# Softmax statistics of two heads side by side in one two-column tile

## The chip, the core and the metric

The kernel runs on one core of a Trainium2 chip. The metric is the device time of one execution in microseconds. TensorE does the matrix products and transposes, VectorE and ScalarE the elementwise work, GpSimd a part of the splits explained below, and SyncE issues the transfers.

## The reference

Two layers work on 256 latent and 256 context tokens of width 1024. Each layer normalises its input, projects it, runs a pooling mixer, a window attention and a global attention, gates and merges the three branches, and ends with a gated MLP. Both attentions have 8 query heads of 64 on 2 key heads. What matters here is the softmax. The window attention has one more logit per head, the sink, which takes part in the maximum and in the sum and has no value:

```python
s_snk = jnp.broadcast_to(sink_l, s_lat.shape[:-1] + (1,))
p = jax.nn.softmax(jnp.concatenate([s_lat, s_ctx, s_snk], axis=-1), axis=-1).astype(v.dtype)
```

The global attention has a plain softmax. Latent queries read latent and context keys, context queries only context keys; the context has no attention of its own in the second layer.

## The kernel before

Matrix products are done in three passes over numbers split into a high and a low part (`mm3`, lines 204 to 207); weights arrive by DMA, ScalarE makes the high part (line 188), GpSimd or VectorE the low part (line 190).

Attention works in units. A unit is one head of one block of 128 queries, and units stand in the order block, key head, `par`, `j`, so that two neighbours (`j` = 0 and 1) are two heads of the same key head and half. They share one tile of split probabilities, and the values are multiplied for both at once. A latent unit has 512 keys, a context unit 256. Layer 0 has 32 units per attention (16 latent, 16 context), layer 1 has 16.

For each unit, `scores` (line 859) makes the scores in a PSUM bank `S` with two products (and a mask product of `triB` for latent window units), takes the negated maximum `nm` on VectorE (line 873), in window attention scales it and takes the smaller of it and the negated sink (line 875), and makes the exponentials `pr` with their row sum `ls` on ScalarE (line 878), in window attention also the sink's exponential `es` (line 883). `finish` (line 886) adds the sink's exponential (line 891), takes the reciprocal `rl` (line 893) and normalises `pr`, on ScalarE for each fourth unit (line 895), otherwise on VectorE (line 897). `turn` (line 899) transposes `pr` on TensorE into `ptp` (line 908) and splits it into `pH` and `pL`; `values` (line 911) multiplies the values of a pair into `O` (line 922).

`S` has two banks, the pool of transposes two, `pr` shares a pool of six tiles, and the small tiles `nm`, `ls`, `es`, `rl` have three buffers each.

`slots` (line 938) lays the steps out in time: slot i holds the scores of unit i and the finish of unit i - 1, then the transposes of unit i - 2 and, each second slot, the values of an earlier pair. `attention` (line 1089) puts other products (the pooling projection, gates, branch projections) between the halves of the slots. From this written order a list scheduler with estimated durations makes the final order of each engine, which is fixed when the program is built. Each engine then works through its own list in order and waits at an instruction whose inputs are not there.

## Time and profile before

| | |
|---|---|
| runs | 1361.81, 1359.25, 1361.93 us, median 1361.81 |
| profiled execution | 1359.41 us, of it the span from first to last instruction 1357.6 us |
| TensorE busy | 1286.9 us, 95% |
| VectorE busy | 900.2 us, 66% |
| ScalarE busy | 661.9 us, 49% |
| GpSimd busy | 568.3 us, 42% |

Shares of the whole span are means over stages that differ; the attention stages take some 280 of the 1357.6 us. Matmuls are pipelined, so that two that follow each other overlap in the busy time. A wait is time in which an engine stood at its next instruction.

### The profile page before, as it was taken

What the parts mean: (1) busy time and instruction counts of PE and PEld (TensorE: products, weight loads), DVE (VectorE), ACT (ScalarE), POOL (GpSimd) and SP (SyncE); (2) the same over time, 40 slices, a digit from 0 to 9 for tenths busy, and PEclk for the clock granted to TensorE, in tenths of its full rate; (3) what the DMA queues carried; (4) which work ended last, traced back from release to release, by engine and by line L of the source; (5) the groups of instructions that cost most, each with busy time, mean ns of one, the idle gap of its engine ahead of it and who ended that gap; (6) DMA issues with size and microseconds to landing.
All of it is one profiled execution on the core that took longest, in us unless ns stands there. A gap on an engine that the chain in (4) does not pass through costs nothing. (4 is left out here: it accounts for less than half of the span.)

```text
span 1357.6 us, 20919 instructions
## 1 busy us (share of the span) xinstructions
PE 1286.9 (95%) x7845; PEld 1125.6 (83%) x7845; DVE 900.2 (66%) x1822; ACT 661.9 (49%) x1216; POOL 568.3 (42%) x317
## 2 busy tenths in 40 slices
PE   4999999999999999999999999998999998999997
PEld 3877778878788888888788788988888888999997
DVE  6879975878767786777755344477847775656522
ACT  5557762557633344333433223456745764555542
POOL 4322223642244425433343443454235325566663
PEclk8999999999999999999999999999999999999999
DMA  9711215432246525644555455544234326577653
GB/s 283 245 40 63 74 51 157 124 94 94 78 153 188 152 82 168 189 141 154 172 171 169 163 163 167 156 140 159 71 107 149 111 78 186 162 212 217 209 173 100
DMA packets 174087, 195.72 MB, mean 144 GB/s; under 512 B 6879, under 2 KB 147831, under 8 KB 173729
## 3 DMA queue, kind: packets, MB, share of 16 engines
q1 hardware_dynamic: 173088, 193.23, 46.0%
q0 software_dynamic: 896, 1.14, 0.4%
q8 instruction: 62, 1.02, 0.3%
q14 instruction: 41, 0.33, 0.1%
HBM read 191.21 MB, written 3.15 MB: 143 GB/s over the span
## 5 line engine op out<-in xcount | busy, mean ns | idle before, releaser
L190 POOL TENSOR_TENSOR wL<-raw,wH 128x1024 fp32r<-128x1024 f32 (+2 forms) x233 | 539.9, 2322 | 741.5 <-ACT wH L188 672.2
L188 ACT ACTIVATE wH<-raw 128x1024 fp32r<-128x1024 f32 (+2 forms) x294 | 293.2, 1001 | 291.2 <-PE gp L206 163.2
L205 PE MATMUL gp<-hH,wH 128*128 128x512 f32 (+1 forms) x1168 | 396.1, 342 | 6.8 <-DVE fa L1257 3.4
L207 PE MATMUL gp<-hH,wL 128*128 128x256 f32 (+1 forms) x1168 | 392.1, 337 | 1.9 <-POOL wL L190 1.4
L206 PE MATMUL gp<-hL,wH 128*128 128x512 f32 (+1 forms) x1168 | 392.2, 337 | 1.8 <-DVE hL L472 1.8
L205 PEld LDWEIGHTS gp<-hH,wH 128*128 128x128 f32 x1168 | 222.3, 191 | 29.6 <-issue 3.4
L207 PEld LDWEIGHTS gp<-hH,wL 128*128 128x128 f32 x1168 | 222.6, 191 | 25.7 <-POOL wL L190 2.5
L206 PEld LDWEIGHTS gp<-hL,wH 128*128 128x128 f32 x1168 | 223.1, 191 | 23.5 <-DVE hL L472 3.3
L433 DVE SCALAR_TENSOR_TENSOR mb<-raw,cs,mb 128x512 f32<-128x512 f32 x196 | 140.7, 751 | 108.5 <-DMA raw<-in_w_mod_dram 107.5
L205 PE MATMUL gp<-g,wH 128*128 128x256 f32 (+1 forms) x396 | 127.3, 322 | 2.4 <-DVE fa L1257 2.4
L206 PE MATMUL gp<-g,wH 128*128 128x256 f32 (+1 forms) x396 | 126.3, 319 | 0.0
L207 PE MATMUL gp<-g,wL 128*128 128x256 f32 (+1 forms) x396 | 126.3, 319 | 0.0
L190 DVE TENSOR_TENSOR wL<-raw,wH 128x1024 fp32r<-128x1024 f32 (+2 forms) x61 | 71.1, 1169 | 74.6 <-ACT wH L188 74.5
L205 PEld LDWEIGHTS gp<-g,wH 128*128 128x128 f32 x396 | 74.5, 188 | 8.9 <-issue 1.6
L207 PEld LDWEIGHTS gp<-g,wL 128*128 128x128 f32 x396 | 74.6, 188 | 6.0
L206 PEld LDWEIGHTS gp<-g,wH 128*128 128x128 f32 x396 | 74.6, 188 | 5.8
L878 ACT ACTIVATE pr<-S,nm 128x512 f32<-128x512 f32 (+1 forms) x96 | 59.4, 619 | 37.0 <-DVE nm L873 15.5
L873 DVE TENSOR_REDUCE nm<-S 128x1 f32<-128x512 f32 (+1 forms) x96 | 56.9, 593 | 21.5 <-PE S L867 12.7
L205 PE MATMUL gp<-y,wH 128*128 128x512 f32 (+1 forms) x192 | 66.7, 349 | 3.5 <-ACT gt L1023 1.5
L206 PE MATMUL gp<-y,wH 128*128 128x512 f32 (+1 forms) x192 | 65.3, 341 | 0.0
L207 PE MATMUL gp<-y,wL 128*128 128x512 f32 (+1 forms) x192 | 65.1, 339 | 0.0
L202 DVE TENSOR_TENSOR pL<-ptp,pH 128x512 fp32r<-128x512 f32 (+1 forms) x96 | 57.0, 596 | 11.1 <-ACT pH L201 10.3
(214 smaller groups left out, 2208.7 us busy)
## 6 DMA issues: line engine op xcount, KB each, us to landing
raw<-in_w_mod_dram SPq DMA_DIRECT2D x80, 512.0 KB, 3.7
raw<-in_w_gate_dram SPq DMA_DIRECT2D x48, 512.0 KB, 3.5
raw<-in_w_ff_gate_dram SPq DMA_DIRECT2D x44, 512.0 KB, 4.2
raw<-in_w_ff_val_dram SPq DMA_DIRECT2D x44, 512.0 KB, 4.4
raw<-in_w_ff_down_dram SPq DMA_DIRECT2D x44, 512.0 KB, 3.6
raw<-in_w_in_dram SPq DMA_DIRECT2D x32, 384.0 KB, 3.2
raw<-in_w_branch_dram SPq DMA_DIRECT2D x24, 512.0 KB, 3.5
raw<-in_w_mod_dram SPq DMA_DIRECT2D x32, 256.0 KB, 5.9
```

What stands on the lines that cost most here:

```text
L188: h = act.activation(out=self.H, in_=self.raw, func=AF.Copy)
L190: lo = eng.tensor_tensor(out=self.L, in0=self.raw, in1=self.H.bitcast(F32), op=ALU.subtract)
L202: dve.tensor_tensor(out=Lo, in0=src, in1=H.bitcast(F32), op=ALU.subtract)
L205: recent.append(pe.matmul(o, lhsT=aH, rhs=bH, start=first, stop=False))
L206: pe.matmul(o, lhsT=aH, rhs=bL, start=False, stop=False)
L207: pe.matmul(o, lhsT=aL, rhs=bH, start=False, stop=last)
L433: dve.scalar_tensor_tensor(out=S["a"][s], in0=raw, scalar=cs[:, s, k:k + 1], in1=S["a"][s], op0=ALU.mult, op1=ALU.add)
L873: dve.tensor_reduce(out=nm, in_=S, axis=AX.X, op=ALU.max, negate=True)
L878: act.activation(out=pr[:, :nkey], in_=S, func=AF.Exp, scale=0.125 if self.window else 1.0, bias=nm, accum_out=ls)
```

## The change

Statistics are kept for two neighbouring units at a time: `nm`, `ls` and `es` are tiles of two columns, one column per unit.

In window attention the first unit of a pair stops after its maximum. After the second unit's maximum, one SCALAR_TENSOR_TENSOR scales both columns and takes the smaller of them and the two negated sinks; then both exponentials are issued, and the sink exponentials of both are made as one VectorE addition and one exponential. Before, the sink was the bias of the exponential. In global attention each unit's exponential is issued at its own maximum as before.

The finish of a pair is issued once, in the slot after the second unit's scores: one addition (window only), one reciprocal of two columns, in place, and the two normalisations. Transposes and values stay in their slots.

```diff
@@ -869,28 +869,38 @@
                 if msk:
                     ob = (1 - t) * P
                     pe.matmul(S[:, ob:ob + P], lhsT=identb, rhs=triB[:, t], start=False, stop=True)
-                nm = small(1, "nm", 3)
-                dve.tensor_reduce(out=nm, in_=S, axis=AX.X, op=ALU.max, negate=True)
+                if j == 0:
+                    self.two = small(2, "nm", 3), small(2, "ls", 3), [], []
+                nm, ls, prs, Ss = self.two
+                dve.tensor_reduce(out=nm[:, j:j + 1], in_=S, axis=AX.X, op=ALU.max, negate=True)
+                prs.append(tmp(name="pr"))
+                Ss.append(S)
                 if self.window:
-                    dve.tensor_scalar(nm, nm, 0.125, nsink[:, l, h:h + 1], op0=ALU.mult, op1=ALU.min)
-                pr = tmp(name="pr")
-                ls = small(1, "ls", 3)
-                act.activation(out=pr[:, :nkey], in_=S, func=AF.Exp, scale=0.125 if self.window else 1.0, bias=nm,
-                               accum_out=ls)
-                es = None
+                    if j == 0:
+                        return
+
+                    dve.scalar_tensor_tensor(out=nm, in0=nm, scalar=0.125, in1=nsink[:, l, h - 2:h + 1:2],
+                                             op0=ALU.mult, op1=ALU.min)
+                for q in range(2) if self.window else (j,):
+                    act.activation(out=prs[q][:, :nkey], in_=Ss[q], func=AF.Exp, scale=0.125 if self.window else 1.0,
+                                   bias=nm[:, q:q + 1], accum_out=ls[:, q:q + 1])
                 if self.window:
-                    es = small(1, "es", 3)
-                    act.activation(out=es, in_=nm, func=AF.Exp, bias=sinkP[:, l, h:h + 1])
-                self.st[i] = (pr, ls, es)
+                    es = small(2, "es", 3)
+                    dve.tensor_tensor(out=es, in0=nm, in1=sinkP[:, l, h - 2:h + 1:2], op=ALU.add)
+                    act.activation(out=es, in_=es, func=AF.Exp)
+                    self.two += (es,)
+                if j == 1:
+                    self.st[i - 1], self.st[i] = self.two, self.two
 
             def finish(self, i):
                 t, kv, par, j = self.units[i]
                 nkey = self.dims(t)[1] * P
-                pr, ls, es = self.st[i]
-                if self.window:
-                    dve.tensor_tensor(out=ls, in0=ls, in1=es, op=ALU.add)
-                rl = small(1, "rl", 3)
-                dve.reciprocal(rl, ls)
+                ls, prs = self.st[i][1:3]
+                if j == 0:
+                    if self.window:
+                        dve.tensor_tensor(out=ls, in0=ls, in1=self.st[i][4], op=ALU.add)
+                    dve.reciprocal(ls, ls)
+                pr, rl = prs[j], ls[:, j:j + 1]
                 if i % 4 in ANORMS:
                     act.activation(out=pr[:, :nkey], in_=pr[:, :nkey], func=AF.Copy, scale=rl)
                 else:
@@ -899,7 +909,7 @@
             def turn(self, i):
                 t, kv, par, j = self.units[i]
                 lat, nkt, koff = self.dims(t)
-                pr = self.st.pop(i)[0]
+                pr = self.st.pop(i)[2][j]
                 if j == 0:
                     self.st["p", i // 2] = [atile([P, 4, 2, P], F32R, f"p{x}", 2) for x in "HL"]
                 pH, pL = self.st["p", i // 2]
@@ -942,8 +952,8 @@
                     a, b = [], []
                     if i < n:
                         a.append(lambda i=i: self.scores(i))
-                    if 1 <= i <= n:
-                        a.append(lambda i=i: self.finish(i - 1))
+                    if i >= 2 and i % 2 == 0 and i <= n:
+                        a.append(lambda i=i: (self.finish(i - 2), self.finish(i - 1)))
                     if 2 <= i <= n + 1:
                         b.append(lambda i=i: self.turn(i - 2))
                     if i >= 4 and i % 2 == 0:
```

The number of TensorE, GpSimd and SyncE instructions is unchanged. VectorE has 72 instructions fewer and ScalarE 24. The final order differs only in the attention stages.

On VectorE, in the last units of layer 0's window attention with context queries (256 keys), these rows stand before; `nm` is the maximum, `ls` the row sum, `rl` its reciprocal, `pr` the probabilities, `pL` the low part of their transposes:

```order
L891 TENSOR_TENSOR ls<-ls,es 128x1
L893 RECIPROCAL rl<-ls 128x1
L891 TENSOR_TENSOR ls<-ls,es 128x1
L897 TENSOR_SCALAR pr<-pr,rl 128x256
L893 RECIPROCAL rl<-ls 128x1
L897 TENSOR_SCALAR pr<-pr,rl 128x256
L202 TENSOR_TENSOR pL<-ptp,pH 128x2x128
L873 TENSOR_REDUCE nm<-S 128x1
L875 TENSOR_SCALAR nm<-nm,nsink 128x1
```

And these now, near the same place:

```order
L875 TENSOR_REDUCE nm<-S 128x1
L882 SCALAR_TENSOR_TENSOR nm<-nm,nsink 128x2
L889 TENSOR_TENSOR es<-nm,sinkP 128x2
L901 TENSOR_TENSOR ls<-ls,es 128x2
L902 RECIPROCAL ls<-ls 128x2
L907 TENSOR_SCALAR pr<-pr,ls 128x256
L875 TENSOR_REDUCE nm<-S 128x1
```

Each unit had its own addition and reciprocal; now the additions, the reciprocal and the scaled maximum are one for two units, and the addition stands behind the second unit's maximum.

On TensorE, in layer 1's window attention, the scores of a unit stood alone before, between other products (`gp`), the transposes (`ptp`) and the values (`O`) of earlier units:

```order
L908 MATMUL ptp<-ident,pr 128x128 x4
L922 MATMUL O<-pH,V 128x256 x4
L922 MATMUL O<-pL,V 128x256
L205 MATMUL gp<-hH_99,wH 128x256
L206 MATMUL gp<-hL_107,wH 128x256
L207 MATMUL gp<-hH_99,wL 128x256
L922 MATMUL O<-pL,V 128x256 x3
L867 MATMUL S<-kT,qT 128x512 x2
L871 LDWEIGHTS identb
L871 MATMUL S<-triB,identb 128x128
```

Now, a little further on in the same stage, there are places where the scores of two units stand closely one behind the other:

```order
L867 MATMUL S<-kT,qT 128x512 x2
L871 LDWEIGHTS identb
L871 MATMUL S<-triB,identb 128x128
L932 MATMUL O<-pH,V 128x256 x4
L932 MATMUL O<-pL,V 128x256 x4
L867 MATMUL S<-kT,qT 128x512 x2
L871 LDWEIGHTS identb
L871 MATMUL S<-triB,identb 128x128
L205 MATMUL gp<-hH_104,wH 128x256
L918 MATMUL ptp<-ident,pr 128x128 x4
```

Only the values of an earlier pair stand between the two units' scores there, and the next transposes follow after one product. In the context part of layer 0 the matmuls keep their order nearly row for row.

## Rows read from the trace of the kernel before

**Rows 1.** The page: busy time of TensorE (share of the span, instructions), and the clock that TensorE was granted, in tenths of full speed, in 40 slices of the span.

```profile
PE 1286.9 (95%) x7845; PEld 1125.6 (83%) x7845; DVE 900.2 (66%) x1822; ACT 661.9 (49%) x1216; POOL 568.3 (42%) x317
...
PEclk8999999999999999999999999999999999999999
```

**Rows 2.** Busy time of each engine in six stretches: window attention of layer 0 with latent and with context queries, global attention of layer 0 with both, window and global attention of layer 1. Columns: stretch, its length, busy us of each engine (instructions), granted clock, share of the DMA engines, GB/s.

```profile
97.00:154.00 57.00, 52.47 (x289) 40.65 (x289) 54.11 (x125) 42.83 (x99) 16.13 (x13) 1.00 0.20 66
154.00:202.00 48.00, 46.07 (x255) 38.20 (x253) 37.79 (x121) 31.76 (x93) 12.63 (x6) 1.00 0.20 56
284.00:327.00 43.00, 41.71 (x243) 34.98 (x242) 33.90 (x71) 32.34 (x70) 12.23 (x12) 1.00 0.30 99
327.00:362.00 35.00, 33.98 (x198) 28.47 (x197) 27.57 (x79) 24.12 (x66) 7.22 (x3) 1.00 0.20 61
941.00:996.00 55.00, 50.28 (x388) 44.86 (x388) 46.17 (x109) 39.78 (x93) 16.90 (x7) 1.00 0.28 85
1064.00:1106.00 42.00, 38.62 (x283) 34.97 (x282) 37.90 (x76) 32.57 (x72) 8.16 (x4) 1.00 0.28 88
```

**Rows 3.** Waits: who waited for whom, us in total, times, longest. The first row is of the whole run, the second of TensorE from 97 to 202, the third of VectorE from 941 to 996.

```profile
PE ptp L908 <- DVE pr L897: 3.6, 3, 1.6
...
PE ptp L908 <- DVE ls L891: 0.2, 1, 0.2
...
DVE nm L873 <- PE S L871: 7.7, 4, 6.5
```

**Rows 4.** VectorE instructions of the whole run, grouped by line and shape: count | busy us, mean ns of one | idle before; the last row is the line of the normalisations, with shortest, median and longest ns of both shapes.

```profile
L873 DVE TENSOR_REDUCE nm<-S 128x1 f32<-128x512 f32 x64 | 43.6, 682 | 19.0 <-PE S L867 10.3 <-PE S L871 8.5
...
L893 DVE RECIPROCAL rl<-ls 128x1 f32<-128x1 f32 x96 | 14.9, 157 | 7.2 <-ACT pr L878 6.2
...
L897 DVE TENSOR_SCALAR pr<-pr,rl 128x256 f32<-128x256 f32 x24 | 10.6, 442 | 0.3
...
L875 DVE TENSOR_SCALAR nm<-nm,nsink 128x1 f32<-128x1 f32 x48 | 9.9, 206 | 0.2
...
L897 DVE TENSOR_SCALAR pr<-pr,rl x72: 335/478/2485, 101.9 to 1104.6; 128x512 f32<-128x512 f32 x48, 128x256 f32<-128x256 f32 x24
```

**Rows 5.** ScalarE instructions of the whole run, grouped in the same way: the exponentials of 512 keys and the sink exponentials.

```profile
L878 ACT ACTIVATE pr<-S,nm 128x512 f32<-128x512 f32 x64 | 44.2, 691 | 22.7 <-DVE nm L873 12.2 <-DVE rl L893 5.3 <-DVE nm L875 4.8
...
L883 ACT ACTIVATE es<-nm,sinkP 128x1 f32<-128x1 f32 x48 | 14.0, 291 | 4.0 <-DVE nm L875 4.0
```

**Rows 6.** Small VectorE instructions: shortest, median and longest ns of the addition of the sink's exponential (line 891) and of the scaled maximum (line 875); the group of a SCALAR_TENSOR_TENSOR on four columns; the addition's busy time in three stretches; and GpSimd's splits (line 190) in these three together.

```profile
L891 DVE TENSOR_TENSOR ls<-ls,es x48: 143/155/2360, 99.7 to 994.9; 128x1 f32<-128x1 f32 x48
...
L875 DVE TENSOR_SCALAR nm<-nm,nsink x48: 191/206/218, 98.4 to 992.9; 128x1 f32<-128x1 f32 x48
...
L455 DVE SCALAR_TENSOR_TENSOR mod<-mred,cols_a 128x4 f32<-128x4 f32 x10 | 7.3, 731 | 0.1
...
L891 DVE TENSOR_TENSOR ls<-ls,es 128x1 f32<-128x1 f32 x48 | 23.2, 483 | 9.4 <-ACT es L883 9.1 <-ACT pr L878 0.2
...
97.00:154.00 57.00, 6.82 (x15) 1.00 0.20 66
154.00:202.00 48.00, 6.55 (x18) 1.00 0.20 56
...
sum 160.00, DVE 2.43 POOL 45.39; mean DVE 0.81 POOL 15.13
```

**Rows 7.** The timeline of a pair of context units in layer 0's window attention: start us, us, engine, line, instruction [idle before, and what ended it]. The first two rows are the scores of the two units, the last is the transposes of the first.

```profile
167.34 0.49 PE L867 MATMUL S<-kT,qT 128*128 128x256 f32 x2
...
169.72 0.40 PE L867 MATMUL S<-kT,qT 128*128 128x256 f32 x2
...
170.59 0.41 DVE L873 TENSOR_REDUCE nm<-S 128x1 f32<-128x256 f32 x1
...
171.18 0.21 DVE L875 TENSOR_SCALAR nm<-nm,nsink 128x1 f32<-128x1 f32 x1
171.24 2.40 POOL L190 TENSOR_TENSOR wL<-raw,wH 128x1024 fp32r<-128x1024 f32 x1 [6.30 <-ACT wH L188]
...
171.42 0.47 ACT L878 ACTIVATE pr<-S,nm 128x256 f32<-128x256 f32 x1 [0.26 <-DVE nm L875]
...
171.89 0.28 ACT L883 ACTIVATE es<-nm,sinkP 128x1 f32<-128x1 f32 x1
...
172.20 1.45 DVE L891 TENSOR_TENSOR ls<-ls,es 128x1 f32<-128x1 f32 x1 [0.81 <-ACT es L883]
...
173.69 0.17 DVE L893 RECIPROCAL rl<-ls 128x1 f32<-128x1 f32 x1
...
173.85 0.38 PE L908 MATMUL ptp<-ident,pr 128*128 128x128 f32 x2
```

**Rows 8.** The timeline of layer 1's window attention: two products of 256 columns that follow each other, the scores of one unit, and the same unit's normalisation.

```profile
944.02 0.28 PE L205 MATMUL gp<-hH,wH 128*128 128x256 f32 x1
...
944.14 0.28 PE L206 MATMUL gp<-hL,wH 128*128 128x256 f32 x1
...
945.10 0.63 PE L867 MATMUL S<-kT,qT 128*128 128x512 f32 x2
...
950.85 0.49 DVE L897 TENSOR_SCALAR pr<-pr,rl 128x512 f32<-128x512 f32 x1
```

## The prediction

> **What bounds the kernel now.** Read the engine totals first. TensorE is busy 1286.9 of 1357.6 us, at full clock nearly everywhere [rows 1]. So VectorE or ScalarE work can only matter where TensorE waits, or where these two engines are nearly full. Next, cut the attention into its six stretches [rows 2]: window attention of layer 0 on the latent queries (97 to 154) and on the context queries (154 to 202), global attention of layer 0 on the same two (284 to 327, 327 to 362), and window and global attention of layer 1 (941 to 996, 1064 to 1106). The reader is to see three kinds of stretch. From 97 to 154 VectorE is busy 54.11 of 57.00 us, 95%, and TensorE 92%: VectorE sets the pace. From 154 to 202 and in both global stretches of layer 0 TensorE is at 96 to 97%. In layer 1 neither is full: TensorE 91 to 92%, VectorE 84 and 90%, and they take turns waiting. The waits are short: in the whole run the transposes of probabilities wait 3.6 us for their normalisation, and only 0.2 us for row sums from 97 to 202, while VectorE waits 7.7 us for scores in the layer 1 window stretch [rows 3].
>
> **What is removed.** A pair of window heads had six small VectorE instructions, two each of TENSOR_SCALAR (206 ns), the sink addition (155 ns at its median) and the reciprocal (157 ns) [rows 4, 6]. It now has four: one SCALAR_TENSOR_TENSOR, two additions, one reciprocal. With the removed kinds' durations that is 2x206 + 2x155 + 2x157 = 1036 ns before and about 206 + 2x155 + 157 = 673 ns after, 363 ns less per pair. Layer 0 has 16 window pairs, layer 1 has 8: 8.7 us. Each pair also saves one sink exponential of 291 ns on ScalarE [rows 5], 7.0 us. A global pair saves one reciprocal, 24 x 157 ns = 3.8 us. What of it lies on the path: in 97 to 154, eight pairs, 2.9 us of VectorE; in layer 1 up to 2.9 us (window) and 1.3 us (global); in the TensorE-bound stretches nothing, for the products hide it.
>
> **What is added: a longer chain before a fixed deadline.** Before, a head's exponential needed only its own maximum. Now, in window attention, the first head's exponential waits for the second head's scores, maximum and SCALAR_TENSOR_TENSOR; then two exponentials run one behind the other; and both heads' reciprocals, in window and global attention, wait for the second row sum. The order on TensorE hardly moves in the context part: its matmuls stand at the same places to within a few rows. So the first head's transposes keep their place while what they wait for comes later.
>
> Take one context pair from the trace [rows 7]. The first head's scores start at 167.34, the second's start at 169.72 and end about 170.12. The first head's transposes start at 173.85. So from the end of the second scores 3.7 us are left, where the first head had 6.0 us of its own before (from the end of its scores near 167.83). The second head's chain, as traced: maximum at 170.59, TENSOR_SCALAR at 171.18, exponential at 171.42, sink exponential 0.47 us behind it, addition at 172.20, which took 1.45 us instead of 0.155, and reciprocal at 173.69. Without the 1.3 us the reciprocal is at 172.39. The second exponential in the chain adds 0.47, then 0.19 us to the normalisation and 0.34 us for it (the 256-key normalisation takes 335 ns at its least; 442 is the mean of all, [rows 4]): 173.39, in time by 0.46 us. With the delay it is 174.69, late by 0.84 us. Before, both cases were hidden by some 2 us of spare time.
>
> So in 154 to 202 the price is that of delays which were free until now. There the additions took 6.55 us for 18, of which 18 x 0.155 = 2.8 is work and 3.8 delay [rows 6]; less 0.46 us of spare in about three pairs that is 2.4 us. I take +2.5. From below it is 0 (no delay meets the chain), from above 6 (one more maximum of 0.41 us in front of each of eight chains, 3.3, on top).
>
> In 97 to 154 the spare time is larger (the order puts 7 to 12 us of products between a pair's last scores and its first transposes, counted at 0.23 us each, twice the 0.12 us between starts of the 256-column ones [rows 8]), so VectorE's work decides: -2.9 us, and about +1.4 for more instructions that can be delayed (there the additions took 6.82 us, 4.5 of it delay, for 15; three such instructions stand where two stood, which is +2.2 if each is as exposed, and less since two of the three follow each other). I take -1.5, bounds -4 and +3.
>
> In the layer 1 window stretch the order leaves 4.5 to 7.7 us, 5.8 on average, counted at 0.12 us per 256-column product. A head traced there had its scores from 945.10 to 945.73 and its normalisation done at 951.34 [rows 8]: 5.6 us, of which some 2.6 is work (0.68 maximum, 0.21, 0.69, 0.29, 0.155, 0.16, 0.48). A second exponential makes 6.3, 0.5 us late; eight times 4 us, against 2.9 us of VectorE work saved. I take +1.5, bounds -2.9 and +5.
>
> In global attention only the reciprocal waits longer: maximum, exponential, reciprocal and normalisation are 0.68 + 0.69 + 0.16 + 0.48 = 2.0 us of work plus hand-overs, and the order leaves 2.5 to 6.1 us after the second scores in layer 0 and 3.7 to 6.2 in layer 1. A chain queued by 1.5 to 2 us, as in the stretches above, is late in the tighter pairs. I take +1 for each layer; bounds 0 to 5 (layer 0, whose saved reciprocals nobody waits for) and -1.3 to +6.
>
> **The port, row and rule.** The sink addition, two small operands in SBUF, took 143 ns at least and 2360 at most, while the TENSOR_SCALAR on the same column never took over 218, though GpSimd ran its splits of 2.4 us beside both [rows 6, 7]. In the traced pair the addition ends when GpSimd's split does (173.64). The Trainium skill (SBUF — State Buffer, the section on its two physically separate sides) says why: VectorE instructions with two SBUF inputs and GpSimd's take a shared port pair as an exclusive lock, and the loser blocks fully. The trace agrees. By that rule the SCALAR_TENSOR_TENSOR that replaces the TENSOR_SCALAR becomes an instruction that can be blocked, in front of both exponentials. A row of such a form is the SCALAR_TENSOR_TENSOR of 128x4, 731 ns on average [rows 6].
>
> **Sum.** 2.5 - 1.5 + 1.5 + 1 + 1 = +4.5 us. The profiled execution took 1359.4 us, 1.8 around its span of 1357.6; the runs' median is 1361.8. These and the other runs lie within 1359.25 to 1361.93, so I add to the mean of all four, 1360.6: **1365.1 us**.
>
> **Rivals.** *The port is the larger price* (slower). If the new SCALAR_TENSOR_TENSOR and addition of sinks are each delayed as the old addition was, mean 483 against 155 ns, that is 24 pairs x (3 - 2) x 0.33 = 7.9 us more on VectorE; where it blocks both exponentials, TensorE waits for most of it: 1360.6 + 7.9 less the part (a third) in the TensorE-bound stretch, plus the 2.5 there = 1368. For it: 45 us of GpSimd splits lie in these stretches. Against it: a split is hit once, whichever instruction comes first.
>
> *VectorE's relief is what counts* (faster). All of the work removed in 97 to 154 and in layer 1 shortens those stretches: -2.9 - 2.9 - 1.3 and, in layer 1, half of 2.3 us of ScalarE: about 1352.5 at the most, 1356 if two thirds count. For it: 95% busy. Against it: only 57 us are that full. It decides if the delays fall where chains have 7 us of spare time.
>
> *Nothing to be measured*: TensorE is 95% busy, products fill in, small gains and losses cancel: 1360.6.
>
> **How the numbers follow.** Forecast 0.38, port 0.12, no change 0.28, relief 0.22. A difference of 0.2%, 2.7 us, is about what can be told from none. The forecast's and the port's cases are slower (0.50), relief faster (0.22), the rest the same (0.28). The forecast's own range is 1362 to 1371; over all cases 8 in 10 lie in 1356 to 1371.
>
> **What would show it.** The context window stretch (48 us before) lengthens by 2 to 3 us, with waits of its transposes for normalised probabilities that were 0.2 us there; the SCALAR_TENSOR_TENSOR's longest is near 2 us; 97 to 154 shortens by 1 to 2. If the waits of transposes do not grow, the chain argument is wrong. If the layer 1 window stretch shortens, relief wins there. If a wait is long enough for the granted clock to fall below the 1.00 of these stretches [rows 2], the loss is larger than worked out.

## The result, and the profile after

The changed kernel takes 1372.61 us (median of four runs, 1370.01 to 1374.09); the kernel before, on the same chip, 1361.87 (1359.25 to 1362.61). The ratio is 1.0078, 95% interval 1.0063 to 1.0094: 10.7 us slower, where 4.5 were forecast and 1371 was the end of the range.

The page of the changed kernel: busy time of the engines, and the granted clock in 40 slices.

```profile
PE 1291.5 (94%) x7845; PEld 1128.4 (82%) x7845; DVE 896.5 (65%) x1750; ACT 655.8 (48%) x1192; POOL 566.9 (41%) x317
...
PEclk8999999999999999999999999999999999999998
```

Against [rows 1], VectorE has 72 instructions fewer and only 3.7 us less busy time. Removing work should have taken 12.5 us off it (8.7 + 3.8). Added up instruction by instruction, the softmax's own lines fell by 15.6 us and all of VectorE by 10.5: other lines rose by 5, and the rest is the overlap of neighbours, which busy time counts once. The six stretches of [rows 2], at their new places, columns as there:

```profile
97.00:161.00 64.00, 54.57 (x289) 40.61 (x288) 55.30 (x111) 40.61 (x91) 17.23 (x13) 0.97 0.18 61
161.00:211.50 50.50, 45.48 (x250) 37.67 (x250) 36.34 (x102) 29.27 (x85) 11.38 (x5) 1.00 0.18 51
293.00:336.00 43.00, 42.63 (x244) 35.34 (x243) 31.47 (x62) 32.53 (x70) 12.00 (x12) 1.00 0.30 99
336.00:370.00 34.00, 32.91 (x193) 27.71 (x191) 25.43 (x69) 23.64 (x63) 7.20 (x3) 1.00 0.20 63
947.50:1009.00 61.50, 52.98 (x391) 47.37 (x390) 46.01 (x93) 37.91 (x85) 16.89 (x8) 0.97 0.25 76
1077.00:1119.00 42.00, 38.59 (x280) 34.82 (x279) 37.53 (x69) 32.98 (x71) 8.13 (x4) 1.00 0.22 74
```

The latent window stretch takes 64.0 us instead of 57.0, its context part 50.5 instead of 48.0, the layer 1 window 61.5 instead of 55.0; global attention loses nothing. In the first, VectorE fell from 95% to 86% busy: its work alone no longer sets the pace.

The cuts of a stretch are chosen by eye. For comparing kernels I count the matmuls in the trace and take the time between the starts of the same ones (both traces have 7845): 450 to 811 and 811 to 1010 are layer 0's window attention, its latent and context parts; 1010 to 1560 the projections behind it; 1560 to 1960 its global attention; 4740 to 5170 and 5640 to 5935 layer 1's window and global attention. In us:

| kernel | window 0, latent | window 0, context | projections | global 0 | window 1 | global 1 |
|---|---|---|---|---|---|---|
| before | 70.6 | 38.5 | 106.2 | 76.6 | 60.2 | 43.6 |
| after | 78.2 | 41.4 | 104.1 | 75.2 | 66.3 | 43.6 |

So +7.6, +2.9, -2.1, -1.4, +6.1 and 0. (The profiled executions differ by 13.4 us, more than the medians, since that of before took 1359.41; outside these six stages the two differ by less than 1 us in all.)

Waits of TensorE in the whole run of the changed kernel, then, behind the line of dots, of VectorE and of TensorE from 947.5 to 1009; us in total, times, longest:

```profile
PE ptp L918 <- DVE pr L907: 13.3, 9, 2.0
PE S L867 <- ACT pr L885: 4.1, 4, 1.5
PE O L932 <- DVE pL L202: 3.1, 3, 1.6
PE ptp L918 <- DVE es L889: 1.9, 1, 1.9
...
DVE nm L875 <- PE S L871: 13.3, 9, 6.6
PE ptp L918 <- DVE pr L907: 7.0, 4, 2.0
```

The transposes' wait for normalised probabilities, 3.6 us in three before [rows 3], is 13.3 in nine; VectorE's wait for scores in layer 1 grew from 7.7 to 13.3. And scores now wait for the exponentials that still read their bank of `S`, 4.1 us in four. The trace shows in front of each of the four a SCALAR_TENSOR_TENSOR that was held; held means here that an instruction lasts until a split of GpSimd beside it is done. The lines behind it, with shortest, median and longest ns:

```profile
L882 DVE SCALAR_TENSOR_TENSOR nm<-nm,nsink x24: 133/154/2212, 101.9 to 1004.0; 128x2 f32<-128x2 f32 x24
  ACT pr L885: 22.5, 14
...
L889 DVE TENSOR_TENSOR es<-nm,sinkP x24: 143/152/165, 102.1 to 1004.2; 128x2 f32<-128x2 f32 x24
...
L901 DVE TENSOR_TENSOR ls<-ls,es x24: 148/152/2298, 105.7 to 1007.1; 128x2 f32<-128x2 f32 x24
```

The row below the SCALAR_TENSOR_TENSOR is who waits for it: ScalarE's exponentials, 22.5 us in 14 cases. The addition of the sinks, right behind an instruction that has waited the split out, is never held (165 ns at the longest). The SCALAR_TENSOR_TENSOR is 154 ns at its median, below the 206 of the TENSOR_SCALAR that it replaced [rows 6], but up to 2212. By lines and shapes (count | busy us, mean ns | idle before):

```profile
L882 DVE SCALAR_TENSOR_TENSOR nm<-nm,nsink 128x2 f32<-128x2 f32 x24 | 12.3, 511 | 0.2
L889 DVE TENSOR_TENSOR es<-nm,sinkP 128x2 f32<-128x2 f32 x24 | 3.7, 153 | 0.3
L885 ACT ACTIVATE pr<-S,nm 128x512 f32<-128x512 f32 x64 | 43.8, 689 | 17.4 <-DVE nm L882 11.4 <-DVE nm L875 5.3 <-DVE ls L902 0.3
```

24 of them take 12.3 us, where 48 TENSOR_SCALAR took 9.9 [rows 4]. One such hold in the timeline, layer 1's window attention (start us, us, engine, line, instruction, [idle before and what ended it]):

```profile
963.39 2.36 POOL L190 TENSOR_TENSOR wL<-raw,wH 128x1024 fp32r<-128x1024 f32 x1 [10.40 <-ACT wH L188]
963.44 0.15 DVE L902 RECIPROCAL ls<-ls 128x2 f32<-128x2 f32 x1
963.56 2.21 DVE L882 SCALAR_TENSOR_TENSOR nm<-nm,nsink 128x2 f32<-128x2 f32 x1
965.69 0.87 DVE L907 TENSOR_SCALAR pr<-pr,ls 128x512 f32<-128x512 f32 x2
965.86 0.69 ACT L885 ACTIVATE pr<-S,nm 128x512 f32<-128x512 f32 x1 [2.55 <-DVE nm L882]
966.31 0.63 PE L918 MATMUL ptp<-ident,pr 128*128 128x128 f32 x4 [2.03 <-DVE pr L907]
...
966.54 0.68 ACT L885 ACTIVATE pr<-S,nm 128x512 f32<-128x512 f32 x1
```

GpSimd's split runs from 963.39 to 965.75. The SCALAR_TENSOR_TENSOR begins inside it and ends with it, at 965.77. Two things stand behind it: both exponentials of its own pair, and, because VectorE goes through its list in order, the normalisation of the pair before, whose reciprocal was ready at 963.59. TensorE waits 2.03 us for that one.

The new instruction is not the only one that is held. The normalisation, a TENSOR_SCALAR on 256 or 512 columns, was held before (2485 ns at the longest, [rows 4]) and still is. Its line after the change, and one case from layer 1's window:

```profile
L907 DVE TENSOR_SCALAR pr<-pr,ls x72: 336/475/2611, 111.1 to 1116.3; 128x512 f32<-128x512 f32 x48, 128x256 f32<-128x256 f32 x24
...
998.31 2.37 POOL L190 TENSOR_TENSOR wL<-raw,wH 128x1024 fp32r<-128x1024 f32 x1 [4.10 <-DVE ls L901]
...
998.51 2.45 DVE L907 TENSOR_SCALAR pr<-pr,ls 128x512 f32<-128x512 f32 x1
...
1001.10 0.63 PE L918 MATMUL ptp<-ident,pr 128*128 128x128 f32 x4 [1.87 <-DVE pr L907]
```

Going through TensorE's waits of over 0.7 us in the three stages that grew, one finds the following. In the context part there are three, 2.6 us together, each behind one of its three held SCALAR_TENSOR_TENSOR. In layer 1's window there are five: 4.7 us behind three held SCALAR_TENSOR_TENSOR and 3.8 behind two held normalisations. In the latent part none of the ten SCALAR_TENSOR_TENSOR is held (163 ns at the longest); there 7.2 us of waits follow two held normalisations, a held addition `ls` and two held instructions that make `qn`.

### The profile page after: what moved, and what is told of

Its sections match the earlier page's. It is cut to its first block, busy times and chain, and to the rows that moved or that the text cites. A ratio compares the mean times of both kernels' runs of the same rounds, so it can differ in the third digit from the quotient of the medians.

```text
span 1371.1 us, 20816 instructions
## 1 busy us (share of the span) xinstructions
PE 1291.5 (94%) x7845; PEld 1128.4 (82%) x7845; DVE 896.5 (65%) x1750; ACT 655.8 (48%) x1192; POOL 566.9 (41%) x317
## 5 line engine op out<-in xcount | busy, mean ns | idle before, releaser
L885 ACT ACTIVATE pr<-S,nm 128x512 f32<-128x512 f32 (+1 forms) x96 | 58.8, 617 | 31.6 <-DVE nm L882 22.5
L918 PE MATMUL ptp<-ident,pr 128*128 128x128 f32 x320 | 51.9, 278 | 16.2 <-DVE pr L907 13.3
```

The source lines that it names most:

```text
L885: act.activation(out=prs[q][:, :nkey], in_=Ss[q], func=AF.Exp, scale=0.125 if self.window else 1.0, bias=nm[:, q:q + 1], accum_out=ls[:, q ...
L918: pe.transpose(pt[:, k], pr[:, k * P:(k + 1) * P], ident)
```

## The experiments

The theory on record was that the longer chain (two units' scores before the first exponential, two row sums before the first reciprocal) meets transposes that stay where they were. The rival was the port: the new SCALAR_TENSOR_TENSOR is an instruction that GpSimd's splits can hold, and the TENSOR_SCALAR was not. Later a third reading was tried: the fixed order that the scheduler made. Ratios are to the kernel before on the same chip, with 95% intervals.

**Which attention.** The first run keeps the pairs in window attention and lets global attention finish unit by unit; the second does the reverse, its window units working by themselves on a column of the shared tiles.

```diff
 e1: finish()
+                if not self.window:
+                    dve.reciprocal(ls[:, j:j + 1], ls[:, j:j + 1])
+                elif j == 0:
...
 e2: scores()
+                    dve.tensor_scalar(nm[:, j:j + 1], nm[:, j:j + 1], 0.125, nsink[:, l, h:h + 1],
+                                      op0=ALU.mult, op1=ALU.min)
```

> Pairs in window attention alone; global units finish one by one as before. By the traces the changed kernel lost about 9 us in layer 0's and 6 us in layer 1's window stage and gained about 2 us in layer 0's global stage. If the window pairs are the whole loss and the stages add up: 12 to 15 us slower than before (ratio 1.009 to 1.011). If pairs in global attention had a share in the loss: under 10 us.

> Pairs in global attention alone: one reciprocal and a joint finish; window units scale, exponentiate and finish one by one, on columns of shared tiles. If the stages add up: 0 to 3 us faster than before (ratio 0.998 to 1.000), layer 0's global stage 2 us shorter. If sharing two-column tiles costs something by itself (a wait between the columns): the window stages are longer than before although their work is that of before.

Window pairs alone: 1382.91 us against 1364.03, ratio 1.0127 (1.0092 to 1.0162), more than the 1.009 to 1.011 expected. Global pairs alone: 1364.06, 0.9995 (0.9981 to 1.0009). The loss is in the window attention. Global attention's stretch in layer 0 is 75.2 us in the second as after the change, 76.6 in the first as before: 1.4 us gained, no more.

**Joint exponentials or joint finish.** The third run exponentiates each window unit at its own maximum, as before, and keeps the joint finish. The fourth keeps the joint exponentials and has neither of the two new two-operand instructions in front of the sums.

```diff
 e3: scores(); finish() and slots() as after the change
+                    dve.tensor_scalar(nm[:, j:j + 1], nm[:, j:j + 1], 0.125, nsink[:, l, h:h + 1],
+                                      op0=ALU.mult, op1=ALU.min)
...
-                for q in range(2) if self.window else (j,):
...
 e4: scores()
-                    dve.scalar_tensor_tensor(out=nm, in0=nm, scalar=0.125, in1=nsink[:, l, h - 2:h + 1:2],
-                                             op0=ALU.mult, op1=ALU.min)
+                    for q in range(2):
+                        dve.tensor_scalar(nm[:, q:q + 1], nm[:, q:q + 1], 0.125, nsink[:, l, h - 2 + 2 * q:h - 1 + 2 * q],
+                                          op0=ALU.mult, op1=ALU.min)
...
-                    dve.tensor_tensor(out=es, in0=nm, in1=sinkP[:, l, h - 2:h + 1:2], op=ALU.add)
-                    act.activation(out=es, in_=es, func=AF.Exp)
+                    for q in range(2):
+                        act.activation(out=es[:, q:q + 1], in_=nm[:, q:q + 1], func=AF.Exp,
+                                       bias=sinkP[:, l, h - 2 + 2 * q:h - 1 + 2 * q])
```

> As the changed kernel, but in window attention each unit scales its own maximum and is exponentiated at once, with the sink as bias; only the finish is joint. If the wait of the first exponential for the second maximum is the loss: 0 to 4 us slower than before. If the joint finish with transposes half a slot behind it is the loss: 8 to 12 us slower, with waits of transposes for normalised probabilities as long as in the changed kernel (13 us in all).

> As the changed kernel, with the coupled exponentials and the joint finish, but two TENSOR_SCALAR instead of the SCALAR_TENSOR_TENSOR and the sinks as bias of two exponentials instead of an addition. If GpSimd blocking these two is the loss: at most 4 us slower than before. If the longer chain is: 10 us slower or more, since VectorE and ScalarE have more to do.

Own exponentials: 1365.30, 1.0004 (0.9986 to 1.0023); its transposes wait 10.8 us for normalised probabilities, which had been expected only together with a loss. Joint exponentials without the two instructions: 1368.08, 1.0027 (1.0011 to 1.0043), at the edge of the 4 us expected. The joint chain stands in the fourth unshortened, and about two thirds of the loss are gone. That speaks against the chain. It doesn't fall yet, since a quarter of a per cent is left.

**More time for the chain.** The fifth run moves the window's transposes one slot later and its values two; the sixth issues the window's joint finish right behind the second unit's scores.

```diff
 e5: slots()
+                d = 1 if self.window else 0
...
-                    if 2 <= i <= n + 1:
-                        b.append(lambda i=i: self.turn(i - 2))
...
+                    if 2 + d <= i <= n + 1 + d:
+                        b.append(lambda i=i: self.turn(i - 2 - d))
+                    if i >= 4 + 2 * d and i % 2 == 0:
+                        b.append(lambda i=i: self.values((i - 4) // 2 - d))
...
 e6: slots()
+                    if self.window:
+                        if i % 2 == 1 and i < n:
+                            a.append(lambda i=i: (self.finish(i - 1), self.finish(i)))
```

> As the changed kernel, with the transposes of window units one slot and their values two slots later in the written order, so that a pair's chain has a slot more. If late chains at the transposes are the main loss (13 us of waits for normalised probabilities in the changed kernel): 0 to 4 us slower than before, with under 4 us of such waits. If the loss lies at the scores (banks freed late, VectorE held in front of the exponentials): 8 us slower or more.

> As the changed kernel, but the joint finish of a window pair is written right behind its second unit's scores, ahead of the next unit's scores. If normalisation is late because VectorE takes the next maximum first: 3 to 6 us of the 10.7 come back. If the order of the finish does not matter, since it waits for the row sums anyway: 9 to 12 us slower than before.

Later transposes: 1378.73 against 1365.63, 1.0092 (1.0069 to 1.0115). Finish at once: 1374.38, 1.0064 (1.0039 to 1.0090), between its two expectations. A chain that is late against its transposes would have been cured by a slot more. It was not, though the transposes' waits for normalised probabilities fell from 13.3 to 4.6 us.

**One of the two instructions.** The seventh run is the changed kernel with two TENSOR_SCALAR for the SCALAR_TENSOR_TENSOR, the eighth with two sink exponentials for the addition of the sinks (the two halves of the fourth's edit).

```diff
 e7: scores()
-                    dve.scalar_tensor_tensor(out=nm, in0=nm, scalar=0.125, in1=nsink[:, l, h - 2:h + 1:2],
-                                             op0=ALU.mult, op1=ALU.min)
+                    for q in range(2):
+                        dve.tensor_scalar(nm[:, q:q + 1], nm[:, q:q + 1], 0.125, nsink[:, l, h - 2 + 2 * q:h - 1 + 2 * q],
+                                          op0=ALU.mult, op1=ALU.min)
...
 e8: scores()
-                    dve.tensor_tensor(out=es, in0=nm, in1=sinkP[:, l, h - 2:h + 1:2], op=ALU.add)
-                    act.activation(out=es, in_=es, func=AF.Exp)
+                    for q in range(2):
+                        act.activation(out=es[:, q:q + 1], in_=nm[:, q:q + 1], func=AF.Exp,
+                                       bias=sinkP[:, l, h - 2 + 2 * q:h - 1 + 2 * q])
```

> As the changed kernel, with two TENSOR_SCALAR in place of the SCALAR_TENSOR_TENSOR only; sinks stay one addition and one exponential. e4 (both replaced) took 0.27% more than before against 0.78%. If GpSimd holding the SCALAR_TENSOR_TENSOR (8.7 us of delay in the changed kernel's window stages) is what e4 took away: again 0.2 to 0.4% slower than before, layer 1's window stage at 61 us against 66. If it was the addition and joint exponential: 0.6 to 0.8%.

> As the changed kernel, with the SCALAR_TENSOR_TENSOR kept and the sinks as bias of two exponentials. If the SCALAR_TENSOR_TENSOR being held is the loss: 0.6 to 0.9% slower than before. If the addition of the sinks and its exponential in the chain were: 0.2 to 0.4%.

Without the SCALAR_TENSOR_TENSOR: 1365.38, 0.9993 (0.9977 to 1.0009). Without the addition: 1375.73, 1.0074 (1.0050 to 1.0098). One instruction decides. The seventh kernel's groups, columns as above, and two waits in it:

```profile
L883 DVE TENSOR_SCALAR nm<-nm,nsink 128x1 f32<-128x1 f32 x48 | 9.6, 204 | 0.3
...
L890 DVE TENSOR_TENSOR es<-nm,sinkP 128x2 f32<-128x2 f32 x24 | 11.3, 470 | 0.4
...
L886 ACT ACTIVATE pr<-S,nm 128x512 f32<-128x512 f32 (+1 forms) x96 | 59.1, 618 | 20.5 <-DVE nm L883 10.0 <-DVE nm L875 8.5 <-PE ptq L830 0.9
...
PE ptp L919 <- DVE pr L908: 10.7, 8, 2.5
```

With the SCALAR_TENSOR_TENSOR away, the addition of the sinks meets the splits: 470 ns instead of 153, 11.3 us in all, nearly what the other took. And the median is no longer than that of before. So it is not the time held that costs, but what is behind it: the instruction that is held no longer stands ahead of the exponentials, which wait 10.0 us for their scaled maxima here and 22.5 in the changed kernel. No wait of TensorE over 0.6 us follows a held addition of the sinks.

Two things limit this reading. The trace is of the slowest of the seventh kernel's ten runs, 1371.16 us. And its layer 1 window takes 65.0 us, where 61 were expected: three normalisations are held there, with 5.7 us of TensorE's waits behind them, and part of it ran at half the clock (below). Held normalisations do cost, with or without the new instruction.

**The instruction without the pairs.** The ninth run is the kernel before, unit by unit, with one edit. The tenth and eleventh are the sixth and fifth with the edit of the seventh.

```diff
 e9: scores() of the kernel before
-                    dve.tensor_scalar(nm, nm, 0.125, nsink[:, l, h:h + 1], op0=ALU.mult, op1=ALU.min)
+                    dve.scalar_tensor_tensor(out=nm, in0=nm, scalar=0.125, in1=nsink[:, l, h:h + 1],
+                                             op0=ALU.mult, op1=ALU.min)
...
 e10: e6, e11: e5, each with the edit of e7
-                    dve.scalar_tensor_tensor(out=nm, in0=nm, scalar=0.125, in1=nsink[:, l, h - 2:h + 1:2],
-                                             op0=ALU.mult, op1=ALU.min)
+                    for q in range(2):
+                        dve.tensor_scalar(nm[:, q:q + 1], nm[:, q:q + 1], 0.125, nsink[:, l, h - 2 + 2 * q:h - 1 + 2 * q],
+                                          op0=ALU.mult, op1=ALU.min)
```

> The kernel before, unit by unit and without pairs, with a SCALAR_TENSOR_TENSOR on one column in place of the TENSOR_SCALAR that scales the maximum. If the SCALAR_TENSOR_TENSOR, held by GpSimd in front of an exponential, is the loss of itself: it is held for 6 to 12 us in all and the kernel is 0.4 to 0.9% slower than before. If it costs only with the coupled exponentials behind it: under 0.3%.

> e6 (finish at once, 0.64% slower) with two TENSOR_SCALAR in place of its SCALAR_TENSOR_TENSOR. If the SCALAR_TENSOR_TENSOR is the loss in any written order: at most 0.3% slower than before. If e7's recovery was the luck of one order: 0.5% or more.

> e5 (later transposes, 0.92% slower) with two TENSOR_SCALAR in place of its SCALAR_TENSOR_TENSOR. If the SCALAR_TENSOR_TENSOR is the loss in any written order: e5's 13 us fall by 6 us or more, to 0.5% or less. If not: still 0.7% or more.

The ninth: 1374.43 against 1365.36, 1.0070 (1.0054 to 1.0087). With no pair anywhere, one changed instruction costs 9 us, nearly all that the change costs. Its rows in that kernel, who waits for it, and by shape its group and that of the old addition:

```profile
L875 DVE SCALAR_TENSOR_TENSOR nm<-nm,nsink x48: 133/151/2077, 99.7 to 1003.2; 128x1 f32<-128x1 f32 x48
  ACT pr L879: 21.2, 14
...
L875 DVE SCALAR_TENSOR_TENSOR nm<-nm,nsink 128x1 f32<-128x1 f32 x48 | 16.3, 339 | 0.2
L892 DVE TENSOR_TENSOR ls<-ls,es 128x1 f32<-128x1 f32 x48 | 16.0, 333 | 11.0 <-ACT es L884 10.7
```

The addition's group fell from 23.2 us [rows 6] to 16.0, and the SCALAR_TENSOR_TENSOR takes 16.3 in place of the TENSOR_SCALAR's 9.9. The holds only partly add up; in part they move ahead of the exponential. The tenth, 1368.02, 1.0019 (1.0008 to 1.0030), and the eleventh, 1363.21, 0.9988 (0.9976 to 1.0001), lie 0.45 and 1.0% below their twins with the instruction (1.0064 and 1.0092).

**A version from the parts that pay.** The third run's layer 1 window was 58.0 us (60.2 before), its layer 0 latent part 75.6 (70.6). The twelfth takes the second run and adds the joint finish in layer 1's window only.

```diff
 e12: finish() and slots() of e2
-                if self.window:
+                if self.window and l == 0:
```

> Joint finish in global attention (both layers) and in layer 1's window attention, unit by unit in layer 0's window attention; exponentials at each unit's own maximum, scaled by TENSOR_SCALAR. By the stages of e2 and e3 (layer 0's global stage 1.3 us and layer 1's window stage 2.2 us shorter than before, layer 0's window stage as before): 2 to 4 us faster than before, ratio 0.997 to 0.9985. If those stage gains were chance of one execution: 1.000.

1360.28 against 1365.36, 0.9964 (0.9950 to 0.9978): 5 us faster than before, where 2 to 4 were expected, and, by the two ratios, 1.1% faster than the changed kernel.

**What holds it.** Three runs more have GpSimd write zeros in place of reading two tensors in its splits: the kernel before, the ninth, and the changed kernel. They leave the low parts that GpSimd makes out of the products. They tell a hold by GpSimd's reads from a worse order of the instructions.

```diff
 e13: the kernel before; e14: e9; e15: after the change
-            lo = eng.tensor_tensor(out=self.L, in0=self.raw, in1=self.H.bitcast(F32), op=ALU.subtract)
+            if eng is pool_e:
+                lo = eng.memset(self.L.bitcast(F32), 0.0)
+            else:
+                lo = eng.tensor_tensor(out=self.L, in0=self.raw, in1=self.H.bitcast(F32), op=ALU.subtract)
```

> The kernel before, with GpSimd writing zeros in place of the low parts of the weights that it makes: it reads nothing from SBUF and leaves those low parts out of the products. It is the base for e14 and e15. Whatever theory holds, the additions of the sink (line 894 here) are no longer delayed if the delay comes from GpSimd's reads; if GpSimd's mere work delays them, they are delayed as before (15.7 us in all).

> e9 (SCALAR_TENSOR_TENSOR alone, 0.70% slower than before) with GpSimd writing zeros, which leaves the low parts out that GpSimd makes. If the loss is GpSimd holding the SCALAR_TENSOR_TENSOR: no such instruction over 0.25 us, and at most 0.15% slower than e13. If the loss is the order that the scheduler makes from another estimate for this instruction: 0.5 to 0.8% slower than e13.

> The changed kernel with GpSimd writing zeros, which leaves the low parts out that GpSimd makes. If held instructions are the loss: what remains is what pairs cost without them, 0 to 0.3% slower than e13. If the longer chain of the pairs or the order is: 0.6 to 0.9% slower than e13.

Before: 1306.12 against 1366.77, 0.9553 (0.9534 to 0.9572). With the instruction alone: 1305.90, 0.9553; to the thirteenth 0.9998. With the change: 1309.26, 0.9578 (0.9559 to 0.9596); to the thirteenth 1.0024. Groups of the fourteenth, then rows of the fifteenth:

```profile
L878 DVE SCALAR_TENSOR_TENSOR nm<-nm,nsink 128x1 f32<-128x1 f32 x48 | 7.3, 152 | 0.2
```

```profile
L885 DVE SCALAR_TENSOR_TENSOR nm<-nm,nsink x24: 137/152/163, 93.3 to 954.8; 128x2 f32<-128x2 f32 x24
```

The SCALAR_TENSOR_TENSOR is no longer held (163 ns at the longest), and it costs nothing. Yet the scheduler's order is still the slower kernel's: the one instruction of the ninth run had also changed the order of the matmuls in the latent part and in layer 1's window, and in the window attentions of the fourteenth they stand one for one as in the ninth. The order of the instructions is therefore not the cause. The comparison is not quite clean: normalisations are still held, though for less (1144 ns at the longest in the thirteenth); GpSimd is also done sooner (959 ns for 2452 for one split) and the whole kernel 60 us shorter, so the chains have other surroundings. The group of the thirteenth:

```profile
L191 POOL MEMSET wL<- 128x1024 f32 x198 | 189.6, 959 | 872.2 <-PE gp L210 802.3 <-PE pkv L209 26.2 <-PE pkv L210 20.5
```

The stages of the runs that the next section reads, cut as above (that of e7 from its slowest run):

| kernel | window 0, latent | window 0, context | projections | global 0 | window 1 |
|---|---|---|---|---|---|
| before | 70.6 | 38.5 | 106.2 | 76.6 | 60.2 |
| after | 78.2 | 41.4 | 104.1 | 75.2 | 66.3 |
| e3 (joint finish, own exponentials) | 75.6 | 39.6 | 105.1 | 75.3 | 58.0 |
| e4 (pairs, no new two-operand ops) | 76.8 | 37.9 | 104.1 | 75.3 | 60.7 |
| e7 (pairs, two TENSOR_SCALAR) | 75.2 | 39.4 | 104.2 | 75.3 | 65.0 |
| e9 (instruction alone) | 69.5 | 41.5 | 106.7 | 76.6 | 63.1 |
| e11 (pairs, later transposes, two TENSOR_SCALAR) | 71.9 | 36.0 | 110.1 | 74.1 | 58.1 |
| e12 | 70.6 | 38.5 | 105.7 | 75.2 | 58.0 |

Some of these stages hold stretches at half the clock, that is at 1.2 of 2.4 GHz: 3.4 us of the changed kernel's latent part and 3.4 of its layer 1 window, 10.2 us of e4's latent part, 3.4 of e7's latent part and 6.8 of its layer 1 window, and nothing in the other kernels of this table. At most half of such a stretch is lost. As stretches (columns as in [rows 2]), e4's latent part and e7's layer 1 window, with granted clocks of 0.93 and 0.95:

```profile
97.10:173.90 76.80, 69.14 (x362) 54.06 (x361) 62.09 (x137) 51.96 (x124) 19.54 (x14) 0.93 0.20 62
...
942.80:1007.80 65.00, 58.76 (x432) 53.19 (x431) 46.35 (x102) 41.94 (x90) 20.15 (x9) 0.95 0.28 82
```

## Why the prediction was wrong

The direction was right, and the reason given for it was not. Six kernels contain the SCALAR_TENSOR_TENSOR against splits that read (after, e1, e5, e6, e8, e9): they lose 0.64 to 1.27%. Seven do not (e2, e3, e4, e7, e10, e11, e12): they lie between 0.36% faster and 0.27% slower. The pairs are in both sets. What does part the two sets in the traces is how long ScalarE's exponentials wait for scaled maxima: 20.5 to 23.8 us in the six, 8.9 to 15.2 in the seven (14.2 before).

*Scaled maximum, "about 206".* This is the step that failed. Unhindered, the instruction takes 154 ns; held, up to 2212, with a mean of 511. Its hold was put at nothing in the sum. The prediction saw in the row of 128x4 (731 ns) and in the rule of the Trainium skill (SBUF — State Buffer, SBUF: two separate sides) that it could be held, and left it to a rival with 0.12. The rule agrees with the runs: VectorE with two SBUF inputs is locked out only by a GpSimd instruction that reads SBUF, and with GpSimd writing only, no SCALAR_TENSOR_TENSOR took over 163 ns.

*The rival "port".* It named the right mechanism, and 1368 was nearer than the forecast. Its price was worked out from VectorE's time, 24 x 0.33 = 7.9 us. The runs show that this is not what is paid: e7's addition of sinks is held for as long, and its ten runs are no slower. What is paid is what waits behind the hold: the exponentials (22.5 us in 14 cases, of which TensorE feels 4.1 at the scores) and the preceding pair's normalisations, less what products fill. "A split is hit once, whichever instruction comes first" was about true (in e9 the addition's time fell by 7.2 us as the new instruction's rose), but no reason against the rival: which instruction is hit decides.

*Latent part, -1.5; measured +7.6.* This term failed too, with the wrong sign. Most of it is not the instruction: e3, with own exponentials and only the finish joint, has +5.0 here and no half clock, and e9 -1.1. (Of e4's +6.2 up to 5.1 can be the clock.) So joining the finish in this stretch costs some 5 us, the reverse of "VectorE's work decides". The trace of e3 says for what: TensorE's waits in this part for normalised probabilities, of which there are none before, and the last of the three that stand right behind a normalisation that was itself held:

```profile
PE ptp L912 <- DVE pr L901: 6.0, 4, 1.9
...
156.16 2.38 POOL L190 TENSOR_TENSOR wL<-raw,wH 128x1024 fp32r<-128x1024 f32 x1 [4.54 <-ACT wH L188]
...
156.78 2.04 DVE L901 TENSOR_SCALAR pr<-pr,ls 128x512 f32<-128x512 f32 x1
...
158.97 0.41 PE L912 MATMUL ptp<-ident,pr 128*128 128x128 f32 x2 [1.40 <-DVE pr L901]
```

Three normalisations took 2.40, 1.93 and 2.04 us there; before, one was held (1.13 us) and TensorE did not wait for it. Behind the fourth wait stands an addition held for 2.35 us. Wherever the prediction counts a normalisation it takes 0.34 or 0.48 us, though [rows 4] had 2485 ns as its longest: the joint finish moved normalisations and the addition to where splits meet them. It fits that with short splits this part is 64.4 us in e15 against 64.3 in e13; a version in which normalisations alone can't be held was not tried. With transposes a slot later (e11) +1.3 is left, but its projections take 3.9 us more. In the changed kernel part of the loss comes back: the projections behind are 2.1 us shorter, global attention 1.4.

*Context part, +2.5; measured +2.9.* Right in size by luck, wrong in cause: e4 has the same chain and is 0.6 us shorter than before, and e9 has no pairs and +3.0. Three held SCALAR_TENSOR_TENSOR, with 2.6 us of waits for `S` behind them, are what the trace shows.

*Layer 1 window, +1.5; measured +6.1.* By e4 (+0.5) and e3, the joint finish alone (-2.2, near the -2.9 of work saved), the instruction is the larger part; by the waits it is 4.7 us to 3.8 behind held normalisations, and e7, with these and without the instruction, has +4.8 in its slowest run. Both signs were inside one term.

*Global, +1 and +1; measured -1.4 and 0.* No delay by the joint reciprocal shows; e2 and e12 show the same 75.2 us in layer 0.

*What would show it.* "If the waits of transposes do not grow, the chain argument is wrong": they grew from 3.6 to 13.3 us, and yet it was. The test was too weak: these waits are 10.7 to 11.2 us in e3, e4 and e7, which lose 0.27% at most, and 4.2 to 8.1 in e5, e6, e8 and e9, which lose 0.64 to 0.92%. The clock point came true in a small way: the granted clock is 0.97 in two stretches that had 1.00 [rows 2]. e4 has more of such half-speed stretches (6.8 us at 110.6, 3.4 at 155.0) and loses 0.27%, so this is not the main cost. It may be all of e4's: the mean granted clock of its runs is 0.981 against 0.986 before, which over the whole time is some 6.5 us at the most (an estimate, the difference times 1364 us) for the 4 that it loses. For e9 (0.983 against 0.9855) the same estimate gives under 4 of its 9 us.

*What stays open.* The stages of e9 add up to some 5 us more than before, its runs to 9; the rest lies in other stages, where equal work varies by several us between executions (549.5 to 554.6 between matmuls 1960 and 4740). The 3.1 us of e15 over e13, which are clear of the scatter (in the profiles the context part is 2.1 us longer and layer 1's window 1.6), were not followed further: that much the pairs cost with no SCALAR_TENSOR_TENSOR held. e1 is slower than the changed kernel by more than the 1.4 us of global attention; three of its four runs have a granted clock of 0.979 to 0.981, the fourth 0.986 and 1376.45 us.

## What to carry to other kernels

Before fusing two small VectorE instructions into one, ask which operands the new one reads, what GpSimd reads beside it, and what stands behind it in VectorE's list. An instruction of 0.15 us that can be held for 2 us is dear in front of an exponential and cost nothing that could be measured behind it; a scalar operand from a column, 50 ns slower when unhindered, was the cheaper form here. Ask the same of larger instructions that merely move: here the normalisations met splits at their new places. Measure the parts of a change one by one: some of them (e12) were worth 5 us while the whole cost 11.

## What had not been expected of the hardware

- A SCALAR_TENSOR_TENSOR on one or two columns takes 151 to 154 ns at its median when free, the TENSOR_SCALAR with a column as scalar 206. A sink exponential without a column as bias takes 208 ns for two columns, against 291 on average for one with it [rows 5]:

```profile
L890 ACT ACTIVATE es<-es x24: 198/208/248, 103.5 to 1006.9; 128x2 f32<-128x2 f32 x24
```

- The TENSOR_SCALAR on a column, whose scalar also lies in SBUF, was never held: 203 and 204 ns on average in e4 and e7, beside the same splits. That is so on one column; on 256 or 512 columns, as the normalisation, it is held for up to 2611 ns after the change.
- Making GpSimd write instead of read in its splits took 60 us (4.5%) off the kernel before, at the price of those low parts; that is more than anything done to the softmax gained. How much of it is holds and how much GpSimd's own shorter time is not separated.
